# A hybrid decoder layer: moving the adaLN columns along the weight stream, splitting the late ones in halves, and spreading four residuals

## The chip, the cores and the metric

The kernel runs on one core of one Trainium2 chip. The metric is the device time of one execution in microseconds (us), taken as the median of repeated runs. Of its engines the text names TensorE (PE in the profile, with PEld for its weight loads), VectorE (DVE), ScalarE (ACT), GpSimd (POOL) and SyncE (SP), which issues the transfers.

## The reference, cut to what matters

One layer over 256 tokens of width 2048, batch 1. Each of three sub-layers is modulated by a condition vector c:

```python
cond = silu(c)
mod = cond @ ada_w + ada_b            # 9 x 2048 values: shift, scale, gate for three sub-layers
h = ada_in(x, norm_g[0], sh1, sc1)    # rmsnorm(x) * (1 + scale) + shift
x = x + 0.5 * gt1 * swiglu(h, w_gate[0], w_up[0], w_down[0])      # SwiGLU_1, 5632 wide
h = ada_in(x, norm_g[1], sh2, sc2)
x = x + gt2 * hybrid_mixer(h)         # 8 attention heads || 8 gated delta heads, then @ w_out
h = ada_in(x, norm_g[2], sh3, sc3)
x = x + 0.5 * gt3 * swiglu(h, w_gate[1], w_up[1], w_down[1])      # SwiGLU_2
return rmsnorm(x, final_norm)
```

All numbers are float32. With a batch of one, `mod` is a matrix times one vector: 144 groups of 128 outputs, each a sum over 2048 inputs. The kernel calls one such group a **column**.

## The kernel before

**The weight stream.** All weights but `ada_w` are cut into 128x128 tiles, 5392 of them, and packed in the order of use, 8 tiles to a **block**: 674 blocks of 512 KB. `Stream.next` hands out tiles; at the first tile of a block it issues the transfer to `wraw` on SP, the cast to `whi` on ACT (L127, a shorter float type that the PE multiplies fast) and the remainder `wraw - whi` to `wlo` on DVE (L139). Each tile is multiplied as `whi` and `wlo` in turn, so that the product is as good as float32. `wraw`, `whi` and `wlo` have four buffers each; DVE and ACT can be four blocks ahead of the PE and no further. If a `wlo` is late, the PE waits for it.

**The stages, in blocks.** 0 to 111: gate and up products of the first 28 hidden groups of SwiGLU_1 (tile `pgu`, L572 to L574), taken in pieces (`PIECES`), each summing some of the 16 slices of the input over 8 or 4 hidden groups; a piece's partial sums are copied from PSUM by ACT or added into `acc` by DVE (L587), the last ones go to `tg`, `tu` and `hid` (L590, L591, L523, L507). 112 to 167: the down product of that half. 168 to 263: the other half of SwiGLU_1. 264 to 377: the mixer's input projections, with the heads' own small chains of work in between. 378 to 409: the output projection `po` (L492, L493), first four output columns of 128 together (8 blocks), then one after the other (2 blocks each). 410 to 673: SwiGLU_2.

**The columns.** `ada_col` fetches one column of `ada_w` (128x2048, 1 MB, tile `adat`, three buffers at most) and DVE multiplies it with `cs` = silu(c) and sums along the row in one instruction (L264, a custom operation and a read of its accumulator). When columns are fetched is a table, `RATE`: pairs of a block and a number of columns per block from there on. A column is also forced where `ada_need` finds it missing. In SwiGLU_1 the sum follows the fetch in the program at once; in the mixer and later (`W.late`) `total` is put off by two blocks (`owing`, `settle`, `BEHIND`) and placed right after a `wlo`. The first 32 columns are scale and shift of SwiGLU_1: each pair makes one slice of its input ready (`gains` L389, L372, L376 or L383), and the pieces ask for the slices in turn.

**The residuals of the output projection.** When an output column is summed in PSUM, `residual` adds it into `x` in two DVE instructions (L516, L517), `sumsq_add` squares it for the next norm, and `norm2.y` makes the next input from it (a gain L389, an ACT copy, and L416 on DVE). The first four columns do this in one go after the fourth (`after`); the later ones one column late, at the ninth slice of the following one (`LATER`).

**What sets the order.** Each engine takes its instructions strictly in the order that the build gives it; a scheduler lays that order out, so a change of `RATE` reorders DVE, ACT, SP and, around the pieces, the PE. An instruction that waits holds up all that stands behind it on its engine.

## Time and profile before

| what | us |
|---|---|
| median of three runs (lowest, highest) | 1944.64 (1944.19, 1946.02) |
| the profiled execution's own time | 1944.91 |
| its span, first to last instruction | 1943.1 |
| PE busy | 1903.0 |
| PEld busy | 1774.5 |
| DVE busy | 1555.1 |
| ACT busy | 1039.5 |

[...] In the lists of instructions a row has its start, its duration, engine, line, operation, the tile written and those read, and in brackets the idle time of its engine before it with what ended it. Rows of the windows view give for a stretch of time the busy time (and the number of instructions) of PE, PEld, DVE, ACT and POOL, then the granted PE clock, the share of time in which the transfer engines were busy, and GB/s.

### The profile page before, as it was taken

What the parts mean: (1) busy time and instruction counts of PE and PEld (TensorE: products, weight loads), DVE (VectorE), ACT (ScalarE), POOL (GpSimd) and SP (SyncE); (2) the same over time, 40 slices, a digit from 0 to 9 for tenths busy, and PEclk for the clock granted to TensorE, in tenths of its full rate; (3) what the DMA queues carried; (4) which work ended last, traced back from release to release, by engine and by line L of the source; (5) the groups of instructions that cost most, each with busy time, mean ns of one, the idle gap of its engine ahead of it and who ended that gap; (6) DMA issues with size and microseconds to landing.
All of it is one profiled execution on the core that took longest, in us unless ns stands there. A gap on an engine that the chain in (4) does not pass through costs nothing.

```text
span 1943.1 us, 33703 instructions
## 1 busy us (share of the span) xinstructions
PE 1903.0 (98%) x13086; PEld 1774.5 (91%) x13087; DVE 1555.1 (80%) x2414; ACT 1039.5 (53%) x1647; POOL 57.4 (3%) x55
## 2 busy tenths in 40 slices
PE   8999999999999999999999999999999999999998
PEld 7999999988999988889989998999999999999997
DVE  6999888989999997789987989877676765666654
ACT  7433555433455446857757655665554445555553
POOL 0000000000000020000000002100000000000011
PEclk9999999999999999999999999999999999999999
DMA  9998867999989985596567567677777766666663
GB/s 374 350 344 345 294 215 265 400 374 376 361 347 348 349 307 211 197 330 219 204 254 250 207 229 281 206 246 264 240 246 262 244 231 199 203 199 202 200 201 120
DMA packets 129490, 519.58 MB, mean 267 GB/s; under 512 B 18217, under 2 KB 21545, under 8 KB 111153
## 3 DMA queue, kind: packets, MB, share of 16 engines
q1 hardware_dynamic: 129330, 517.42, 74.1%
q8 instruction: 103, 1.69, 0.3%
q14 instruction: 57, 0.47, 0.1%
HBM read 512.89 MB, written 4.47 MB: 266 GB/s over the span
## 4 chain that ended last, share of the span: by engine, by line
PE 77%; DVE 12%; issue 4%; ACT 3%; DMA 2%; SPq 0%; DVEq 0%; ACTq 0%
PE pd L492 12%; PE pu L488 10%; PE pg L488 10%; PE pd L493 6%; PE pu L489 5%; PE pg L489 5%; DVE wlo L139 5%; PE pgu L574 4%; PE pgu L572 4%; PE pgu L573 4%; DVE adat L264 3%; PE po L492 2%; PE pp L795 2%; PE pp L796 2%; PE pp L797 2%
## 5 line engine op out<-in xcount | busy, mean ns | idle before, releaser
L139 DVE TENSOR_TENSOR wlo<-wraw,whi 128x1024 fp32r<-128x1024 f32 x674 | 820.8, 1225 | 263.8 <-ACT whi L127 262.6
L127 ACT CAST whi<-wraw 128x1024 fp32r<-128x1024 f32 x674 | 698.3, 1045 | 509.4 <-PE pd L492 178.1
L492 PE MATMUL pd<-hid,whi 128*128 128x512 f32 x1408 | 462.1, 382 | 0.0
L493 PE MATMUL pd<-hid,wlo 128*128 128x256 f32 x1408 | 384.8, 274 | 2.7 <-DVE wlo L139 2.7
L264 DVE CUSTOM_DVE_ANT_0 adat<-adat,cs,colt 128x2048 f32<-128x2048 f32 x142 | 334.6, 2357 | 7.6 <-DMA adat<-in_ada_dram 7.4
L488 PE MATMUL pg<-hs,whi 128*128 128x512 f32 x912 | 302.1, 382 | 0.5 <-DVE shc L439 0.5
L488 PE MATMUL pu<-hs,whi 128*128 128x512 f32 x912 | 302.2, 382 | 0.0
L492 PEld LDWEIGHTS pd<-hid,whi 128*128 128x128 f32 x1408 | 266.0, 189 | 36.7 <-DVE hid L507 0.2
L493 PEld LDWEIGHTS pd<-hid,wlo 128*128 128x128 f32 x1408 | 270.2, 192 | 6.0 <-DVE wlo L139 5.6
L489 PE MATMUL pu<-hs,wlo 128*128 128x256 f32 x912 | 249.3, 273 | 0.0
L574 PE MATMUL pgu<-hs,wlo 128*128 128x256 f32 x896 | 240.7, 278 | 8.3 <-DVE wlo L139 8.0
L489 PE MATMUL pg<-hs,wlo 128*128 128x256 f32 x912 | 248.8, 273 | 0.0
L572 PE MATMUL pgu<-hs,whi 128*128 128x256 f32 x896 | 244.8, 276 | 0.8 <-DVE acc L587 0.5
L573 PE MATMUL pgu<-hs,whi 128*128 128x256 f32 x896 | 244.5, 276 | 0.0
L488 PEld LDWEIGHTS pg<-hs,whi 128*128 128x128 f32 x912 | 172.4, 189 | 24.9 <-ACT shc L438 0.7
L488 PEld LDWEIGHTS pu<-hs,whi 128*128 128x128 f32 x912 | 172.4, 189 | 23.6
L795 PE MATMUL pp<-hs,whi 128*128 128x256 f32 x656 | 188.4, 288 | 1.1 <-ACT hs L379 1.1
L797 PE MATMUL pp<-hs,wlo 128*128 128x256 f32 x656 | 182.2, 278 | 0.0
L796 PE MATMUL pp<-hs,whi 128*128 128x256 f32 x656 | 181.9, 277 | 0.0
L574 PEld LDWEIGHTS pgu<-hs,wlo 128*128 128x128 f32 x896 | 168.8, 193 | 11.0 <-DVE wlo L139 10.8
L489 PEld LDWEIGHTS pu<-hs,wlo 128*128 128x128 f32 x912 | 175.0, 192 | 1.4 <-DVE wlo L139 1.4
L489 PEld LDWEIGHTS pg<-hs,wlo 128*128 128x128 f32 x912 | 175.1, 192 | 0.3
(335 smaller groups left out, 2585.9 us busy)
## 6 DMA issues: line engine op xcount, KB each, us to landing
wraw<-in_w_dram SPq DMA_DIRECT2D x674, 512.0 KB, 4.4
adat<-in_ada_dram SPq DMA_DIRECT2D x142, 1024.0 KB, 7.5
xr<-in_xr_dram SPq DMA_DIRECT2D x4, 512.0 KB, 5.6
adaf<-in_ada_dram SPq DMA_DIRECT2D x4, 512.0 KB, 8.5
xd<-x SPq DMA_DIRECT2D x4, 512.0 KB, 6.9
rw<-rowd SPq DMA_DIRECT2D x16, 128.0 KB, 4.2
x<-xd SPq DMA_DIRECT2D x4, 512.0 KB, 5.6
out_dram<-o SPq DMA_DIRECT2D x8, 256.0 KB, 2.6
```

The source lines that it names most:

```text
L127: self.cast = self.nc.scalar.copy(self.h, r).ins
L139: lo_ = nc.vector.tensor_tensor(self.l, r, self.h.bitcast(F32), ALU.subtract)
L264: V.tensor_tensor_reduce(t, t, cs, 1.0, L("adab", q, 1), ALU.mult, ALU.add, mod[:, q : q + 1])
L488: PE.matmul(ps, wt[0], both, start=(k == 0), stop=False)
L489: PE.matmul(ps[:, T:], wt[1], part(k, HI), start=False, stop=(k == KD - 1))
L492: PE.matmul(ps, wt[0], act.rearrange("p q (a b) -> p q b a", a=2), start=first, stop=False)
L493: PE.matmul(ps[:, :T], wt[1], woven(act[:, 0]), start=False, stop=last)
L572: PE.matmul(o, wh, part(k, HI), start=first and s == 0, stop=False, skip_group_check=skip)
L573: PE.matmul(o, wh, part(k, LO), start=False, stop=False, skip_group_check=skip)
L574: PE.matmul(o, wl, part(k, HI), start=False, stop=last, skip_group_check=skip)
L795: PE.matmul(pp[i][:, :T], wh, hh, start=(k == 0), stop=False)
L797: PE.matmul(pp[i][:, :T], wl, hh, start=False, stop=(k == KD - 1))
```

## The change

Three things change (the edit inside `total` has no effect, since the late columns no longer pass through it). `RATE` is another table: 0.25 instead of 0.45 columns per block in blocks 28 to 32 and 49 to 55, 0.5 instead of 0.45 in blocks 12 to 27, 33 to 48 and 56 to 65, 0.2 instead of about 0.06 in blocks 66 to 111, none from block 376 to 423 (before: none from 404), and 0.16 instead of 0.125 in SwiGLU_2. A late column is summed in two halves of 1024, the second one block after the first; the first half's sum goes through a small tile `part`. And in the output projection every residual is owed singly: while more than one is owed, two are paid per output column (`SLOTS`, at slices 3 and 11), else one at slice 8.

```diff
-RATE = ((0, 0.5), (12, 0.45), (68, 0.06), (112, 0.5), (168, 0.38), (264, 0.0), (284, 0.26), (404, 0.0), (424, 0.125))
+RATE = ((0, 0.5), (28, 0.25), (33, 0.5), (49, 0.25), (56, 0.5), (66, 0.2), (112, 0.5), (168, 0.38), (264, 0.0), (284, 0.255), (376, 0.0), (424, 0.16))
...
+SLOTS = (3, 11)
...
         def total():
-            with nullcontext() if W.late else W.behind(False):
+            with W.behind(False):
                 V.tensor_tensor_reduce(t, t, cs, 1.0, L("adab", q, 1), ALU.mult, ALU.add, mod[:, q : q + 1])
...
         if W.late:
-            W.owing.append((len(W.order) // WB, total))
+            part = tiny.tile([P, 1], F32, name="part", bufs=4)
+            for i, (start, dst) in enumerate(((L("adab", q, 1), part), (part, mod[:, q : q + 1]))):
+                hf = slice(i * D // 2, (i + 1) * D // 2)
+                W.owing.append((len(W.order) // WB + i, lambda hf=hf, start=start, dst=dst: V.tensor_tensor_reduce(
+                    t[:, hf], t[:, hf], cs[:, hf], 1.0, start, ALU.mult, ALU.add, dst)))
         else:
             total()
...
+            slots = SLOTS if len(owed) > 1 else (LATER,)
...
-                if owed and i == LATER:
+                if owed and i in slots:
                     owed.pop(0)()
...
-            def after(js=js, pj=pj):
-                for q, j in enumerate(js):
-                    residual(pj[q], j, 5, False)
-                    sumsq_add(j)
-                    norm2.y(j)
-                    if j == KD // 2:
-                        sqrt_table(x[:, j, :1])
-
-            if j == 3 or j == KD - 1:
-                after()
-            else:
-                owed.append(after)
+            def after(j, ps):
+                residual(ps, j, 5, False)
+                sumsq_add(j)
+                norm2.y(j)
+                if j == KD // 2:
+                    sqrt_table(x[:, j, :1])
+
+            owed += [lambda j=j, ps=ps: after(j, ps) for j, ps in zip(js, pj)]
+        while owed:
+            owed.pop(0)()
         mx.close()
```

How many columns DVE sums in which stretch of the stream in the two built programs (a column belongs to the block behind whose `wlo` it stands, a halved one to that of its second half):

| blocks | 0-12 | 13-27 | 28-32 | 33-48 | 49-55 | 56-65 | 66-111 | 112-263 | 264-377 | 378-409 | 410-673 |
|---|---|---|---|---|---|---|---|---|---|---|---|
| before | 6 | 7 | 2 | 7 | 3 | 5 | 4 | 62 | 24 | 7 | 15 |
| now | 6 | 8 | 1 | 8 | 2 | 5 | 10 | 61 | 23 | 2 | 16 |

The order moves at many places; three bear the prediction. In the changed program the same source lines stand up to five lines lower (L140 is L139 before, L265 is L264, L381 is L376, L394 is L389, L421 is L416, L521 and L522 are L516 and L517, L592 is L587).

First, DVE from the low part of block 26 to that of block 28, in SwiGLU_1. Before:

```order
L139 TENSOR_TENSOR wlo<-wraw,whi 128x1024
L383 SCALAR_TENSOR_TENSOR hs<-ht,mod,hs 128x2x128
L587 TENSOR_TENSOR acc<-pgu,acc 128x512 x4
L139 TENSOR_TENSOR wlo<-wraw,whi 128x1024
L264 ISA adat,mod<-adat,cs,colt 128x2048
L264 ISA mod 128x1
L587 TENSOR_TENSOR acc<-pgu,acc 128x512 x3
L139 TENSOR_TENSOR wlo<-wraw,whi 128x1024 x2
```

Now:

```order
L140 TENSOR_TENSOR wlo<-wraw,whi 128x1024
L592 TENSOR_TENSOR acc<-pgu,acc 128x512 x4
L140 TENSOR_TENSOR wlo<-wraw,whi 128x1024
L265 ISA adat,mod<-adat,cs,colt 128x2048
L265 ISA mod 128x1
L394 SCALAR_TENSOR_TENSOR g_1253<-mod,colt 128x1
L592 TENSOR_TENSOR acc<-pgu,acc 128x512
L377 SCALAR_TENSOR_TENSOR ht<-x,g_1253,nrow 128x256
L592 TENSOR_TENSOR acc<-pgu,acc 128x512 x2
L140 TENSOR_TENSOR wlo<-wraw,whi 128x1024
L381 TENSOR_TENSOR hs<-ht,hs 128x2x128
```

The column and the seven additions into `acc` stand where they stood; a gain and a product for the next input slice have come in front of block 28, and, as the table counts, one more column lies in the blocks ahead.

Second, DVE from the first of the eight additions that end the third piece to the low part of block 50. Before:

```order
L587 TENSOR_TENSOR acc<-pgu,acc 128x512
L139 TENSOR_TENSOR wlo<-wraw,whi 128x1024
L376 TENSOR_TENSOR hs<-ht,hs 128x2x128
L587 TENSOR_TENSOR acc<-pgu,acc 128x512 x4
L139 TENSOR_TENSOR wlo<-wraw,whi 128x1024
L264 ISA adat,mod<-adat,cs,colt 128x2048
L264 ISA mod 128x1
L587 TENSOR_TENSOR acc<-pgu,acc 128x512 x3
L139 TENSOR_TENSOR wlo<-wraw,whi 128x1024 x3
```

Now:

```order
L140 TENSOR_TENSOR wlo<-wraw,whi 128x1024
L592 TENSOR_TENSOR acc<-pgu,acc 128x512
L265 ISA adat,mod<-adat,cs,colt 128x2048
L265 ISA mod 128x1
L592 TENSOR_TENSOR acc<-pgu,acc 128x512 x4
L140 TENSOR_TENSOR wlo<-wraw,whi 128x1024
L592 TENSOR_TENSOR acc<-pgu,acc 128x512 x3
L140 TENSOR_TENSOR wlo<-wraw,whi 128x1024 x2
```

The low part of block 48 has come out from behind the first addition, which waits for the PE; the column has moved from behind the low part of block 49 to in front of it.

Third, DVE from the low part of block 388 on, where the first four output columns are finished (`g` with a number is the gain of one column). Before, with a second pair of L416, half a residual and a gain still to follow before the low part of block 389:

```order
L139 TENSOR_TENSOR wlo<-wraw,whi 128x1024
L516 SCALAR_TENSOR_TENSOR x<-po,mod,x 128x256 x2
L517 SCALAR_TENSOR_TENSOR x<-po,mod,x 128x256 x2
L516 SCALAR_TENSOR_TENSOR x<-po,mod,x 128x256 x2
L416 SCALAR_TENSOR_TENSOR hs<-x,g_13645,hs 128x2x128
L416 SCALAR_TENSOR_TENSOR hs<-x,g_13654,hs 128x2x128
L517 SCALAR_TENSOR_TENSOR x<-po,mod,x 128x256
L389 SCALAR_TENSOR_TENSOR g_13663<-mod,colt 128x1
L517 SCALAR_TENSOR_TENSOR x<-po,mod,x 128x256
L389 SCALAR_TENSOR_TENSOR g_13672<-mod,colt 128x1
L264 ISA adat,mod<-adat,cs,colt 128x2048
L264 ISA mod 128x1
```

Now:

```order
L140 TENSOR_TENSOR wlo<-wraw,whi 128x1024 x2
L521 SCALAR_TENSOR_TENSOR x<-po,mod,x 128x256 x2
L522 SCALAR_TENSOR_TENSOR x<-po,mod,x 128x256 x2
L521 SCALAR_TENSOR_TENSOR x<-po,mod,x 128x256
L140 TENSOR_TENSOR wlo<-wraw,whi 128x1024
L421 SCALAR_TENSOR_TENSOR hs<-x,g_13716,hs 128x2x128
L421 SCALAR_TENSOR_TENSOR hs<-x,g_13747,hs 128x2x128
L522 SCALAR_TENSOR_TENSOR x<-po,mod,x 128x256
L394 SCALAR_TENSOR_TENSOR g_13779<-mod,colt 128x1
L521 SCALAR_TENSOR_TENSOR x<-po,mod,x 128x256
L394 SCALAR_TENSOR_TENSOR g_13810<-mod,colt 128x1
L140 TENSOR_TENSOR wlo<-wraw,whi 128x1024
```

The low part of block 389 now stands behind five halves of residuals, where it stood behind nine of them, four L416, three gains and a column; the rest of the four residuals is spread over the blocks after it. The two columns that remain in this stage are one at its start (its second half) and one, fetched late, with its halves behind the low parts of blocks 407 and 408.

## The prediction, made before the changed kernel had run

> **What bounds the kernel now.** The page's first line says that the PE is busy for 98% of the span. That leaves 40 us, and a busy PE can still be slowed, so the windows view of the stages comes next (PE, PEld, DVE, ACT, POOL busy, granted clock, share of the transfer engines, GB/s).
>
> ```profile
> PE 1903.0 (98%) x13086; PEld 1774.5 (91%) x13087; DVE 1555.1 (80%) x2414; ACT 1039.5 (53%) x1647; POOL 57.4 (3%) x55
> ...
> 50.00:104.00 54.00, 51.17 (x442) 49.70 (x440) 51.98 (x62) 24.62 (x30) 0.00 (x0) 1.00 0.88 342
> 104.00:168.00 64.00, 59.76 (x528) 59.18 (x528) 61.09 (x71) 25.94 (x30) 0.00 (x0) 1.00 0.93 355
> 212.00:331.00 119.00, 119.00 (x1068) 119.00 (x1067) 95.28 (x154) 64.21 (x95) 0.00 (x0) 1.00 0.70 234
> 331.00:483.00 152.00, 149.90 (x920) 136.76 (x919) 143.28 (x169) 61.96 (x64) 0.00 (x0) 1.00 0.98 382
> 800.00:1168.00 368.00, 358.43 (x2680) 337.25 (x2679) 311.65 (x761) 242.33 (x526) 0.42 (x2) 1.00 0.67 240
> 1275.00:1943.00 668.00, 660.29 (x4043) 606.57 (x4041) 430.28 (x552) 325.74 (x452) 17.95 (x14) 1.00 0.65 217
> ```
>
> From 212 to 331 us, in blocks 66 to 111, the PE does not stop: 1068 matmuls in 119 us, 0.111 us each, 24 to a block, so 2.67 us a block is its own pace. Between 50 and 168 us DVE is busy 113 of 118 us and the PE misses 7: there DVE sets the time. SwiGLU_2, the last row, has a third of DVE free. So the change can earn only where DVE is late, and lose only where it is nearly full.
>
> The waits of the PE by itself, in its list of instructions, show the largest in the output projection:
>
> ```profile
> 1175.48 0.38 PE L492 MATMUL po<-oh,whi 128*128 128x512 f32 x1
> ...
> 1177.10 0.48 PE L492 MATMUL po<-oh,whi 128*128 128x512 f32 x1 [0.69 <-ACT whi L127]
> 1179.59 0.38 PE L493 MATMUL po<-oh,wlo 128*128 128x256 f32 x1 [2.01 <-DVE wlo L139]
> 1179.80 0.59 PE L492 MATMUL po<-oh,whi 128*128 128x512 f32 x1
> ...
> 1182.32 0.63 PE L492 MATMUL po<-oh,whi 128*128 128x512 f32 x1
> ...
> 1183.43 0.38 PE L492 MATMUL po<-oh,whi 128*128 128x512 f32 x1
> ```
>
> The PE stops at 1176.4 (1177.10 less 0.69) and gets the one of block 389 at 1179.6: 0.69 + 2.01 = 2.7 us idle. The 0.69 is put down to a cast, but the next row shows that the low part was missing anyway. What DVE did meanwhile:
>
> ```profile
> 1168.02 1.23 DVE L139 TENSOR_TENSOR wlo<-wraw,whi 128x1024 fp32r<-128x1024 f32 x1 [2.70 <-ACT whi L127]
> 1169.17 0.87 DVE L516 SCALAR_TENSOR_TENSOR x<-po,mod,x 128x256 f32<-128x256 f32 x2
> 1169.95 0.86 DVE L517 SCALAR_TENSOR_TENSOR x<-po,mod,x 128x256 f32<-128x256 f32 x2
> 1170.74 0.87 DVE L516 SCALAR_TENSOR_TENSOR x<-po,mod,x 128x256 f32<-128x256 f32 x2
> ...
> 1173.80 2.40 DVE L264 CUSTOM_DVE_ANT_0 adat<-adat,cs,colt 128x2048 f32<-128x2048 f32 x1
> ...
> 1176.07 1.87 DVE L416 SCALAR_TENSOR_TENSOR hs<-x,g,hs 128x256 fp32r<-128x256 f32 x2
> 1178.32 1.21 DVE L139 TENSOR_TENSOR wlo<-wraw,whi 128x1024 fp32r<-128x1024 f32 x1
> ```
>
> Between the low parts of blocks 388 and 389 lie 9.1 us of residuals, L416 and one column. And from 1179.8 to 1183.4 a matmul of 512 columns takes 0.59 to 0.63 us, where it takes 0.38 before and after. The windows tell why:
>
> ```profile
> 170.00:172.00 2.00, 2.00 (x11) 2.00 (x10) 2.00 (x2) 1.05 (x1) 0.00 (x0) 0.50 0.98 342
> 882.00:886.00 4.00, 4.00 (x37) 4.00 (x37) 3.93 (x11) 3.97 (x6) 0.00 (x0) 1.00 0.99 373
> 1180.00:1182.00 2.00, 2.00 (x7) 1.72 (x7) 2.00 (x3) 0.84 (x2) 1.06 (x1) 0.50 0.70 213
> ```
>
> After the wait the granted clock is 0.50, for some 3.4 us of half the work: 1.7 us more. The same happens at 170 us; behind a wait of 1.58 us that ends at 881.89 (its row is below) it does not.
>
> **The change part by part. Output projection.** The column in front of block 389 goes, and of nine halves of residuals five stay (0.40 us each by the rows above: 2.0 us), so its low part ends near 1169.2 + 2.0 + 1.2 = 1172.4, and the PE asks for it at 1176.8: 4 us early. Behind it come two L416 (1.87 together), two halves (0.8) and two gains (0.3), 3.0 us, then 1.1 for the next low part: 4.1 us to the PE's 2.6 a block. The blocks after that hold one L416, two halves and a gain, 2.9 with their low part, and soon only every other block does. The lead falls to about 2.5 us and then grows, since from 394 on two blocks bring DVE 4.0 us of work in 5.2; it is never used up. So the wait and its slow stretch go: **-2.7 - 1.7 = -4.4 us**. At least -2.7 (if the slow stretch has another cause); no more than -4.4, since nothing else waits there. The late column behind blocks 407 and 408, with a wait for its transfer 4.9 us (by the row at 242.07, below), is paid from the lead won by then, six times 1.2.
>
> **SwiGLU_1, the first two stretches.** Here DVE is full and its list is a sum of durations:
>
> ```profile
> 99.15 1.22 DVE L139 TENSOR_TENSOR wlo<-wraw,whi 128x1024 fp32r<-128x1024 f32 x1
> 100.28 2.35 DVE L264 CUSTOM_DVE_ANT_0 adat<-adat,cs,colt 128x2048 f32<-128x2048 f32 x1
> 102.55 1.88 DVE L587 TENSOR_TENSOR acc<-pgu,acc 128x512 f32<-128x512 f32 x3
> 104.35 2.35 DVE L139 TENSOR_TENSOR wlo<-wraw,whi 128x1024 fp32r<-128x1024 f32 x2
> 105.62 0.38 PE L574 MATMUL pgu<-hs,wlo 128*128 128x256 f32 x1 [2.25 <-DVE wlo L139]
> 157.31 0.69 DVE L587 TENSOR_TENSOR acc<-pgu,acc 128x512 f32<-128x512 f32 x1 [2.19 <-PE pgu L574]
> 157.92 1.22 DVE L139 TENSOR_TENSOR wlo<-wraw,whi 128x1024 fp32r<-128x1024 f32 x1
> 159.39 2.48 DVE L587 TENSOR_TENSOR acc<-pgu,acc 128x512 f32<-128x512 f32 x4
> 161.78 1.21 DVE L139 TENSOR_TENSOR wlo<-wraw,whi 128x1024 fp32r<-128x1024 f32 x1
> 162.91 2.34 DVE L264 CUSTOM_DVE_ANT_0 adat<-adat,cs,colt 128x2048 f32<-128x2048 f32 x1
> 165.19 1.88 DVE L587 TENSOR_TENSOR acc<-pgu,acc 128x512 f32<-128x512 f32 x3
> 166.98 3.48 DVE L139 TENSOR_TENSOR wlo<-wraw,whi 128x1024 fp32r<-128x1024 f32 x3
> 168.25 0.38 PE L574 MATMUL pgu<-hs,wlo 128*128 128x256 f32 x1 [2.25 <-DVE wlo L139]
> DVE acc L587 <- PE pgu L574: 3.4, 3, 2.2
> ```
>
> From start to start a column costs 2.27, an addition 0.6, a low part 1.13. The first waits are at block 28 (105.62) and block 50 (168.25).
>
> Block 28: one column more lies ahead of it (2.27) with a gain and a product (0.2 + 0.4), 2.9 us. DVE's own idle ahead of block 28 pays a part: the last row has three waits for additions, 3.4 us; one, of 2.19, is at 157.31, so 1.2 us lie before. The low part comes 2.9 - 1.2 = 1.7 us later and the PE with it. By block 33 both tables have summed 15 columns and DVE is level again, but the PE, which was at its own pace from 28 to 33, stays 1.7 behind.
>
> Block 50: the first of the eight additions waits for the PE, so it comes at 157.31 + 1.7 = 159.0. From there to the end of the low part of block 50 DVE had 168.2 - 157.3 = 10.9 us to do; now the low part of 48 and L376 are done before, 1.13 + 0.4 less: 9.4. It ends at 168.4, 0.2 later than before. The PE's idle time in blocks 48 to 50 shrinks from 2.4 to about 1.2 us.
>
> Then the clock. Of two waits of 2.25 us one (168.25) was followed by a slow stretch and one (105.62) was not; the windows from 104 to 168 show 1.00. [...] The wait at block 28 grows to about 2.9 us, since the PE loses 1 us of the 1.7 ahead of it: I take a slow stretch there (+1.7) and none at block 50 any more (-1.7); the PE's later arrival only moves block 50's wait forward. Together **+0.2 us**. Bounds: -1.5 with neither, +1.9 with both.
>
> [...]
>
> **SwiGLU_1 from block 66, and the down product.** Ten columns instead of four stand in blocks 66 to 111. Six times 2.27 is 13.6 us of DVE; its row of windows leaves 119 - 95.3 = 23.7. Cover: the PE never waited there, though this happened:
>
> ```profile
> 242.07 2.35 DVE L264 CUSTOM_DVE_ANT_0 adat<-adat,cs,colt 128x2048 f32<-128x2048 f32 x1 [2.58 <-DMA adat<-in_ada_dram]
> ```
>
> DVE stood still for 4.9 us for one column, and the lead held. The down product (331 to 483) has DVE at 94% and the transfer engines at 98%, with as many columns as before, and begins with a smaller lead: I take **+0.5 us**; 0 at best, +3 at worst, more than the 2.1 us that the PE misses there now.
>
> **Mixer and SwiGLU_2.** A half costs 1.28 us (the kernel's first columns are summed so):
>
> ```profile
> L710 DVE CUSTOM_DVE_ANT_0 adaf<-adaf,cs,colt x2: 1276/1280/1284, 11.7 to 14.8; 128x1024 f32<-128x1024 f32 x2
> 881.89 0.30 PE L1215 MATMUL pft<-colt,on 128*128 128x128 f32 x1 [1.58 <-issue]
> ```
>
> Two halves take some 0.3 us more than one whole (2 x 1.28 against 2.35, with another read of 0.08): 12 us over 40 columns, hidden in the 56 us that DVE has free from 800 to 1168 and the 238 of SwiGLU_2. Without that cover each would cost its 0.3. What stands behind a late column on DVE waits 1.2 us less. The wait at 881.89 is one for attention's `on`, whose chain on DVE stands behind a column in block 307: **-1.2 us**, if that is all that makes it late; 0 to -2.5 with the other chains.
>
> **The sum**: -4.4 + 0.2 + 0.5 - 1.2 = -4.9. From the profiled execution's 1944.9 that is 1940.0; it lies 0.3 above the median, so the forecast is **1939.7 us**. What this kernel's measurement can tell from no change is about 0.2%, 3.9 us, so 1940.7 is the edge of faster.
>
> **The rivals.** [...]
>
> *Slow at both places and no gain in the mixer*: +1.7 and +1.2 on the forecast, 1942.6. For it: the wait at 881.89 is named "issue" and not DVE.
>
> *The new columns of blocks 66 to 111 wait for their transfers*: if all six cost 2.27 + 2.58 = 4.85, they want 29.1 us of the 23.7 that DVE has free; the PE loses 5.4 and, stopping at each of the last three, three slow stretches of 1.7: 1939.7 + 10.5 = 1950.2, slower than before. It decides from the point where the lead of four blocks is gone, in the last of these blocks, where an L590 group stands in nearly each. Against it: one of four waited so.
>
> *The wait of block 389 only moves*, to 390 or 391, where the low parts stand behind 2.9 us: a stop of 1 us with a slow stretch, +2.7, 1942.4.
>
> [...]
>
> *The change doesn't do what it says*: the columns taken out are forced back in by `ada_need` at the projection's end; the built order has one such, so this is small: 1944.
>
> **Chances.** Forecast 0.42, no slow stretch at 28 0.25, slow at both 0.14, transfers 0.08, moved wait 0.05, page's rule 0.03, undone 0.03. The forecast's own range is 1938 to 1941.5. The range that leaves out about 2 in 10 runs from 1935.5 (the mixer's lower bound with neither slow stretch) to 1943.0 (above the third case). Faster by over 0.2%: nearly all of the second case and five sixths of the first, 0.60; slower: 0.08; within: 0.32.
>
> **What would show it.** Right: no PE wait over 0.5 us and a clock of 1.00 in the output projection; the low part of block 28 near 107 us, that of block 50 near 168; no PE wait from 212 to 331 us; the wait before `pft` near block 307 down to about 0.4. Wrong: a wait of the PE for `wlo` in blocks 389 to 395, a half clock there, PE waits in blocks 95 to 115, or a low part of block 28 that comes no later than 105.6.

## The result, and the profile after

The changed kernel is slower: 1949.2 us (median of 17 runs, 1945.5 to 1953.7) against 1944.64 for the kernel before, whose 17 runs beside it lay between 1941.3 and 1946.3. The ratio is 1.0024, with a 95% interval from 1.0017 to 1.0030. The forecast was 1939.7, in a range from 1935.5 to 1943.0.

The page of the changed kernel has the same 98% of PE as before; what differs is the sum by engine of the chain of waits, and the group of the whole columns (busy time, mean ns, idle time before them):

```profile
PE 1903.0 (98%) x13086; PEld 1776.8 (91%) x13087; DVE 1564.0 (80%) x2496; ACT 1041.6 (53%) x1645; POOL 57.0 (3%) x55
...
PE 74%; DVE 11%; DMA 6%; issue 4%; ACT 3%; SPq 0%; DVEq 0%; ACTq 0%
...
L265 DVE CUSTOM_DVE_ANT_0 adat<-adat,cs,colt 128x2048 f32<-128x2048 f32 x101 | 239.0, 2366 | 18.0 <-DMA adat<-in_ada_dram 18.0
```

Transfers have gone from 2% to 6% of the chain, and DVE stands 18.0 us in front of columns that have not landed (7.4 before, though of 142 columns and not of 101). PE's busy time is to the tenth that of before: all 7.4 us by which the span grew (1950.5 against 1943.1) are idle time of the PE. The profiled execution of the changed kernel took 1952.3 us, 3.1 more than the median, so the stretches below add up to 7.4 us where the medians differ by 4.6. Where the idle time is shows when the moment at which the PE first uses the low part of a block is compared in the two traces. Differences of the changed kernel to the one before, in us, by stretch of blocks (the start of the execution apart, since it moves by up to 2.4 us from one execution to the next):

| stretch | what runs | forecast | measured |
|---|---|---|---|
| start | | | -0.3 |
| 0 to 66 | SwiGLU_1, first stretches | +0.2 | -0.8 |
| 66 to 120 | SwiGLU_1, first down blocks | | **+11.7** |
| 120 to 264 | down product, second half | +0.5 (from 66 on) | +0.3 |
| 264 to 384 | mixer | -1.2 | +1.6 |
| 384 to 408 | output projection | -4.4 | -5.0 |
| 408 to end | SwiGLU_2 | 0 | -0.1 |

The windows that answer to those of before (same columns: PE, PEld, DVE, ACT, POOL busy, clock, share of the transfer engines, GB/s), the third of them over blocks 66 to 111:

```profile
49.70:103.70 54.00, 51.54 (x442) 49.82 (x440) 53.14 (x63) 23.51 (x29) 0.00 (x0) 1.00 0.91 344
103.70:167.70 64.00, 60.28 (x522) 59.90 (x522) 59.29 (x70) 26.33 (x30) 0.00 (x0) 0.97 0.84 326
211.00:345.80 134.80, 126.18 (x1105) 125.12 (x1104) 110.26 (x171) 67.31 (x99) 0.00 (x0) 0.99 0.74 266
341.00:494.00 153.00, 149.13 (x908) 135.44 (x908) 144.76 (x171) 62.16 (x64) 0.00 (x0) 1.00 0.98 384
```

The stretch in which the PE never stopped now takes 134.8 us with 8.6 idle and a clock of 0.99, while DVE has 24 us free. So it is not too little room on DVE; it is when DVE is free. Its list, and that of the PE, give the stops one by one:

```profile
252.78 2.35 DVE L265 CUSTOM_DVE_ANT_0 adat<-adat,cs,colt 128x2048 f32<-128x2048 f32 x1 [0.89 <-DMA adat<-in_ada_dram]
265.33 2.35 DVE L265 CUSTOM_DVE_ANT_0 adat<-adat,cs,colt 128x2048 f32<-128x2048 f32 x1 [2.37 <-DMA adat<-in_ada_dram]
281.02 2.35 DVE L265 CUSTOM_DVE_ANT_0 adat<-adat,cs,colt 128x2048 f32<-128x2048 f32 x1 [3.72 <-DMA adat<-in_ada_dram]
285.24 0.38 PE L579 MATMUL pgu<-hs,wlo 128*128 128x256 f32 x1 [1.66 <-DVE wlo L140]
296.93 2.35 DVE L265 CUSTOM_DVE_ANT_0 adat<-adat,cs,colt 128x2048 f32<-128x2048 f32 x1 [3.92 <-DMA adat<-in_ada_dram]
301.14 0.38 PE L579 MATMUL pgu<-hs,wlo 128*128 128x256 f32 x1 [2.24 <-DVE wlo L140]
312.97 2.35 DVE L265 CUSTOM_DVE_ANT_0 adat<-adat,cs,colt 128x2048 f32<-128x2048 f32 x1 [3.66 <-DMA adat<-in_ada_dram]
317.52 0.38 PE L579 MATMUL pgu<-hs,wlo 128*128 128x256 f32 x1 [1.09 <-DVE wlo L140]
329.15 2.35 DVE L265 CUSTOM_DVE_ANT_0 adat<-adat,cs,colt 128x2048 f32<-128x2048 f32 x1 [2.46 <-DMA adat<-in_ada_dram]
333.36 0.38 PE L579 MATMUL pgu<-hs,wlo 128*128 128x256 f32 x1 [2.17 <-DVE wlo L140]
345.89 0.38 PE L498 MATMUL pd<-hid,wlo 128*128 128x256 f32 x1 [1.56 <-DVE wlo L140]
```

A column every four or five blocks (one more, at 239.85, waited 0.97 and is not listed); the wait of DVE grows from 0.9 to 3.9 us, and from the column at 281.02 on each one reaches the PE: 1.66 + 2.24 + 1.09 + 2.17 = 7.2 us. A last wait of 1.56, at block 112, stands behind a column that had landed in time: by then there was no lead left. Together 8.7 us. After the second of the PE's waits, at 301.14, comes a slow stretch (clock 0.50 at 303, below; from 302.1 to 305.5 the matmuls start 0.21 us apart instead of 0.11), 1.7 us more, which makes 10.4 of the 11.7; no row names the rest.

Where the wait comes from is to be seen on SP and DVE around the column at 296.93 (SPq rows: the issue of transfers; x3 are three in a row):

```profile
285.21 3.34 SPq L125 DMA_DIRECT2D wraw<-in_w_dram  x3
288.60 0.43 SPq L261 DMA_DIRECT2D adat<-in_ada_dram  x1
```

```profile
286.97 1.23 DVE L140 TENSOR_TENSOR wlo<-wraw,whi 128x1024 fp32r<-128x1024 f32 x1
...
288.78 1.22 DVE L140 TENSOR_TENSOR wlo<-wraw,whi 128x1024 fp32r<-128x1024 f32 x1
...
291.78 1.23 DVE L140 TENSOR_TENSOR wlo<-wraw,whi 128x1024 fp32r<-128x1024 f32 x1 [0.52 <-ACT whi L128]
296.93 2.35 DVE L265 CUSTOM_DVE_ANT_0 adat<-adat,cs,colt 128x2048 f32<-128x2048 f32 x1 [3.92 <-DMA adat<-in_ada_dram]
```

The fetch stands on SP behind the transfer of block 100, and that one waits for a raw buffer which DVE frees with the low part of block 95 (286.97 + 1.23 = 288.2; each fifth block has a raw buffer of its own in this stage, so there are five of `wraw` and not four). So the fetch cannot leave before 288.6, whatever SP does. The sum stands on DVE behind the low part of block 97, two low parts on, and DVE is there at 293.0, 4.4 us after the issue. The transfer lands 8.3 us after it (296.9), and DVE stands for the difference, 3.9 us.

The wait grows because the transfers take longer, and not because DVE comes sooner: from the issue to the end of DVE's work ahead of the sum it is 4.6 us at 252.78 and 4.4 at 281.02 and 296.93, while the transfer takes 5.5, 8.1 and 8.3. Nor does a full lead help much: with 5.9 us of it DVE reached the sum at 242.07 in the kernel before 5.6 us after the issue, against a transfer of 8.2, and with 5.8 us the one at 284.37 in k11_dose (below) after 4.3, against 7.6. What stretches the transfers from 5.5 to 8.3 us no run here shows. That DVE stood for nothing is an idle time; that it stood ahead of a low part is the loss.

### The profile page after: what moved, and what is told of

Its sections match the earlier page's. It is cut to its first block, busy times and chain, and to the rows that moved or that the text cites. A ratio compares the mean times of both kernels' runs of the same rounds, so it can differ in the third digit from the quotient of the medians.

```text
span 1950.5 us, 33806 instructions
## 1 busy us (share of the span) xinstructions
PE 1903.0 (98%) x13086; PEld 1776.8 (91%) x13087; DVE 1564.0 (80%) x2496; ACT 1041.6 (53%) x1645; POOL 57.0 (3%) x55
## 4 chain that ended last, share of the span: by engine, by line
PE 74%; DVE 11%; DMA 6%; issue 4%; ACT 3%; SPq 0%; DVEq 0%; ACTq 0%
PE pd L497 14%; PE pg L493 10%; PE pu L493 10%; PE pd L498 7%; PE pu L494 5%; PE pg L494 5%; DVE wlo L140 4%; PE po L497 3%; DMA adat<-in_ada_dram 3%; PE pgu L579 2%; PE pgu L577 2%; PE pgu L578 2%; PE pp L800 2%; PE pp L801 2%; PE pp L802 2%
## 5 line engine op out<-in xcount | busy, mean ns | idle before, releaser
L140 DVE TENSOR_TENSOR wlo<-wraw,whi 128x1024 fp32r<-128x1024 f32 x674 | 821.5, 1226 | 255.6 <-ACT whi L128 253.1
L493 PE MATMUL pu<-hs,whi 128*128 128x512 f32 x912 | 302.1, 382 | 0.0
L579 PE MATMUL pgu<-hs,wlo 128*128 128x256 f32 x896 | 241.4, 279 | 14.7 <-DVE wlo L140 14.3
L265 DVE CUSTOM_DVE_ANT_0 adat<-adat,cs,colt 128x2048 f32<-128x2048 f32 x101 | 239.0, 2366 | 18.0 <-DMA adat<-in_ada_dram 18.0
```

Of the source, the lines that this page charges most:

```text
L140: lo_ = nc.vector.tensor_tensor(self.l, r, self.h.bitcast(F32), ALU.subtract)
L265: V.tensor_tensor_reduce(t, t, cs, 1.0, L("adab", q, 1), ALU.mult, ALU.add, mod[:, q : q + 1])
L493: PE.matmul(ps, wt[0], both, start=(k == 0), stop=False)
L579: PE.matmul(o, wl, part(k, HI), start=False, stop=last, skip_group_check=skip)
```

## The experiments

Twelve kernels ran, each timed in several rounds beside the kernel before, whose median in these rounds was 1944.9, 1945.7 and 1945.5 us. The last columns give the difference to the kernel before by stretch of blocks, from one profiled execution each; in the mixer (264 to 384) they depend on which slow stretches of the clock (0.50 for some 3.4 us, as from 302.1 to 305.5 above), 1.7 us each, that execution had.

| run | median, us | ratio (95%) | 0-66 | 66-120 | 120-264 | 264-384 | 384-408 |
|---|---|---|---|---|---|---|---|
| changed kernel | 1949.2 | 1.0024 (1.0017 to 1.0030) | -0.8 | +11.7 | +0.3 | +1.6 | -5.0 |
| k1_put_off | 1948.9 | 1.0020 (1.0011 to 1.0028) | -0.8 | +11.7 | +0.3 | +0.3 | -5.0 |
| k7_put_off | 1941.7 | 0.9983 (0.9974 to 0.9992) | -1.0 | +2.9 | +0.5 | -3.4 | -5.0 |
| k13_put_off_hole | 1941.7 | 0.9981 (0.9972 to 0.9990) | -0.9 | 0.0 | -1.9 | +1.0 | -5.0 |
| k2_rate66 | 1936.9 | 0.9962 (0.9949 to 0.9974) | -0.8 | 0.0 | -0.5 | -3.3 | -5.0 |
| k11_dose | 1941.7 | 0.9978 (0.9969 to 0.9988) | -0.8 | +1.3 | -0.6 | +2.1 | -5.0 |
| k12_whole | 1948.8 | 1.0019 (1.0009 to 1.0029) | -0.9 | +9.9 | +0.4 | -2.2 | -5.0 |
| k3_residuals | 1945.4 | 1.0002 (0.9993 to 1.0010) | 0.0 | 0.0 | 0.0 | +0.8 | -0.4 |
| k4_out_of_po | 1940.0 | 0.9976 (0.9966 to 0.9987) | 0.0 | +0.2 | 0.0 | -1.6 | -5.0 |
| k5_halves | 1945.4 | 1.0002 (0.9994 to 1.0011) | +0.9 | 0.0 | +0.1 | -2.1 | +0.5 |
| k6_first | 1943.8 | 0.9999 (0.9990 to 1.0008) | -0.9 | +0.3 | -0.6 | +0.8 | -0.3 |
| k9_col28 | 1937.2 | 0.9960 (0.9948 to 0.9972) | -3.9 | 0.0 | -2.0 | +2.6 | -5.0 |
| k10_best | 1933.0 | 0.9939 (0.9926 to 0.9953) | -3.9 | 0.0 | -2.0 | -0.6 | -5.0 |

### Where the sum stands: k1_put_off, k7_put_off, k13_put_off_hole

The first try at putting the sums off, on the changed kernel:

```diff
+        elif m > 1 and len(W.order) // WB < 112:
+            W.owing.append((len(W.order) // WB, lambda: V.tensor_tensor_reduce(...)))
         else:
             total()
```

> The changed kernel, with one thing altered: below block 112 the sum of a column that is not needed yet stands two blocks behind its fetch on DVE, as the late columns' sums do, instead of right at its fetch. Same columns, same places of the fetches, same DVE work. Theory A (each of the new columns of blocks 66 to 111 holds DVE up because it stands on DVE ahead of the landing of its own transfer, about 3.5 us a column): DVE's waits for adat in 212 to 331 us go from 18 us to under 4, the PE's five waits of 1.1 to 2.2 us in blocks 93 to 112 and the half clock at 302 us go, and 10 to 11 us come back: 1938 to 1940. Theory B (DVE has simply too much work there, six columns more of 2.3 us): the waits for adat go but the PE still waits for low parts: no more than 3 us come back, 1946 or more. Theory C (the transfers themselves are late because the queue is full, wherever the sum stands): DVE still waits for adat, only later: 1944 to 1949.

It measured 1948.9, and the waits of the changed kernel are there again. But it tells nothing of the theories: `both` calls `ada_need` at each tile, and that ends with `W.settle()`, which pays all owed sums at once, so the order of DVE was that of the changed kernel. It is of use as a repeat: the same order gave the same 11.7 us, though made up otherwise. The PE waited 7.3 us instead of 8.7 and had two slow stretches instead of one, the second after this wait, which was 2.17 in the changed kernel:

```profile
333.61 0.58 PE L582 MATMUL pgu<-hs,wlo 128*128 128x256 f32 x1 [3.11 <-DVE wlo L140]
```

The wait of 1.56 at block 112 is not there in this execution. That fits a PE that is soon to wait for DVE anyway: what a slow stretch takes from it is then not lost a second time. The mixer has +0.3 instead of +1.6, so 1.3 us there is what one execution differs from another; its wait for `x` before `plog` is 1.34 us here and 2.81 in the changed kernel.

The second try takes that call away where only the first 32 columns can be asked for:

```diff
             ada_col()
-        W.settle()
+        if m > 1:
+            W.settle()
```

> The changed kernel with the sums of blocks 66 to 111 really put off (the run k1_put_off built the order of the changed kernel: an earlier call pays all owed sums at the next tile). Each column is fetched where it was, but its sum stands five low parts later on DVE (behind the low part of block 97 before, now of 102). Same columns, same DVE work, 5 of 9 columns of the stretch still summed there. Theory A (the loss is the standing of the sum ahead of its transfer's landing): DVE's waits for adat from 212 to 331 us fall from 18 us to under 2, no PE wait over 0.5 us in blocks 90 to 112, no half clock at 302 us, 11 to 12 us less than the changed kernel: 1937 to 1939. Theory B (six columns of 2.3 us are too much work): PE waits for low parts stay in blocks 100 to 112, 1944 or more.

The waits are gone, with the same columns in the same places on SP. Windows of this kernel over blocks 66 to 111, and of its end alone, then DVE and the PE one by one:

```profile
211.00:334.00 123.00, 123.00 (x1104) 123.00 (x1103) 108.39 (x169) 67.64 (x99) 0.00 (x0) 1.00 0.81 291
```

```profile
288.66 2.35 DVE L276 CUSTOM_DVE_ANT_0 adat<-adat,cs,colt 128x2048 f32<-128x2048 f32 x1
...
328.41 2.35 DVE L265 CUSTOM_DVE_ANT_0 adat<-adat,cs,colt 128x2048 f32<-128x2048 f32 x1 [0.71 <-DMA adat<-in_ada_dram]
```

```profile
340.04 0.38 PE L502 MATMUL pd<-hid,wlo 128*128 128x256 f32 x1 [2.60 <-DVE wlo L140]
```

DVE does 108.4 us of work in 123 and the PE does not stop once: theory B, too much work, falls, and so does theory C, since DVE waits for a column for no more than the 0.7 us of the row at 328.41. The transfers issued between 270 and 311 us are a little shorter here than in the changed kernel (6.2 to 7.2 us against 8.1 to 8.4), but in the next run, where those issued between 270 and 300 take 8.1 to 8.8, DVE does not wait for them either. What is left is 2.9 us behind block 112, where two columns stand behind the low parts of neighbouring blocks (111 and 112) at the start of the down product. Against the changed kernel the median is 7.5 us lower. The expectation of 11 to 12 was missed: within blocks 66 to 112 all 11.6 us came back, but 2.9 were lost again behind them. To see whether the two columns make the 2.9, the third run leaves blocks 107 to 116 without any:

```diff
-(66, 0.2), (112, 0.5), (168, 0.38), (264, 0.0), (284, 0.255)
+(66, 0.2), (107, 0.0), (117, 0.5), (168, 0.38), (264, 0.0), (284, 0.315)
```

> k7_put_off without columns from block 107 to 116, the mixer at 0.315 to take them over. In k7_put_off two columns stood behind the low parts of 111 and 112, where the down product begins, and the PE waited 2.6 us at block 113. Without them that wait goes, and 66 to 120 costs the PE nothing: 2.5 to 3 us less than k7_put_off: 1938 to 1939.5 by the median, if the mixer takes its columns as it did in k2_rate66.

They do: in the window of this kernel from 211 to 340 us the PE has no gap,

```profile
211.00:340.00 129.00, 129.00 (x1148) 128.71 (x1147) 113.92 (x180) 72.27 (x106) 0.00 (x0) 1.00 0.79 276
```

but the median, 1941.7, did not follow. The mixer, which has to take five columns more, came out 4.4 us worse than in k7_put_off in the profiled executions, and blocks 120 to 264 2.3 better. In the mixer it has a slow stretch at 864 us that k7_put_off did not have and one at 745 that is twice as long; together they are 3.4 us, as much as k7_put_off's whole gain there. The expectation that it would go as in k2_rate66 was wrong.

### How many columns: k2_rate66, k11_dose

```diff
-(66, 0.2), (112, 0.5), (168, 0.38), (264, 0.0), (284, 0.255)
+(66, 0.06), (112, 0.5), (168, 0.38), (264, 0.0), (284, 0.33)
```

> The changed kernel, with the rate of columns in blocks 66 to 111 back at 0.06 and the mixer's raised from 0.255 to 0.33 to take the columns over. Theory A (the loss is these six columns alone): the 11.6 us that are lost in blocks 92 to 112 come back, and the mixer pays for six more halved columns up to 2 us: 1937 to 1940. Theory B (the loss comes from what the first stretches leave behind for blocks 66 to 111, a smaller lead): the waits in blocks 93 to 112 stay, 1946 to 1950.

1936.9, and 0.0 in blocks 66 to 120: the 11.7 us are the columns that were added, and nothing that the earlier stretches leave behind. The mixer takes them for nothing here. The dose between:

```diff
-(66, 0.2), (112, 0.5), (168, 0.38), (264, 0.0), (284, 0.255)
+(66, 0.125), (112, 0.5), (168, 0.38), (264, 0.0), (284, 0.29)
```

> The changed kernel with a column every 8 blocks (0.125) instead of every 5 (0.2) in blocks 66 to 111, the rest in the mixer (0.29 instead of 0.255); the sums stand ahead of their transfers as in the changed kernel. If a stop of DVE (2.3 us of sum and up to 3.7 us of waiting) is paid back at about 0.8 us a block, 8 blocks pay it and 5 do not: the PE then waits in blocks 66 to 112 for less than 1 us in all and 10 to 12 us come back: 1936 to 1940. If any wait for adat of 2 us and more reaches the PE, half of the loss stays: 1943 to 1945.

DVE still stands in front of its columns, and the PE does not notice (two rows of DVE, then the window):

```profile
284.37 2.35 DVE L265 CUSTOM_DVE_ANT_0 adat<-adat,cs,colt 128x2048 f32<-128x2048 f32 x1 [3.29 <-DMA adat<-in_ada_dram]
304.76 2.35 DVE L265 CUSTOM_DVE_ANT_0 adat<-adat,cs,colt 128x2048 f32<-128x2048 f32 x1 [2.17 <-DMA adat<-in_ada_dram]
```

```profile
211.00:334.00 123.00, 123.00 (x1103) 122.97 (x1102) 101.10 (x161) 65.35 (x97) 0.00 (x0) 1.00 0.74 259
```

The lead of DVE, from the end of a low part to its first use, tells why (us, best before a stop and least behind it, from the two traces; four stops in a row, in the changed kernel from that at 239.85, in k11_dose from that at 262.50):

| | first | second | third | fourth |
|---|---|---|---|---|
| changed kernel, every 5 blocks | 5.3 to 1.6 | 5.4 to 2.7 | 4.7 to 0.5 | 3.8, PE waits 1.7 |
| k11_dose, every 8 blocks | 5.8 to 1.5 | 5.8 to 1.1 | 5.8 to 1.1 | 4.3 to 0.4 |

A stop costs some 3 to 5 us of lead, and the blocks up to the next one win back 2 to 4 where there are five, and all of it, to the full 5.8, where there are eight, but for the last (4.3). By the median k11_dose came out at 1941.7, above the 1936 to 1940 expected: 1.3 us went up to block 120, 0.9 of it in a wait at block 115, and the mixer lost 2.1.

### The output projection: k3_residuals, k4_out_of_po

The first has the columns of the kernel before and the residuals one by one, that is the last three pieces of the change alone; the second the residuals in one go and the columns out, that is a table alone:

```diff
# k3_residuals, on the kernel before
+            slots = SLOTS if len(owed) > 1 else (LATER,)
...
+            owed += [lambda j=j, ps=ps: after(j, ps) for j, ps in zip(js, pj)]
# k4_out_of_po, on the kernel before
-(284, 0.26), (404, 0.0), (424, 0.125)
+(284, 0.33), (376, 0.0), (424, 0.16)
```

> The kernel before, with the residuals of the output projection owed one by one and nothing else: its columns as before, whole and in the projection too. If the wait of block 389 came from the residuals standing in one go (4 us of them ahead of the low part), it goes with its slow stretch, and 4 to 5 us are won: 1940. If the column of 2.3 us ahead of block 389 is needed for the wait, about half of the wait stays: the low part of 389 comes some 2 us earlier, the PE still waits 0.5 to 1 us, with or without a slow stretch: 1941 to 1943.5.

> The kernel before with a table that has no columns from block 376 to 423 and 0.33 instead of 0.26 in the mixer; whole columns, residuals in one go. It asks what the columns alone do in the output projection, where the residuals alone gave 0.4 us (k3_residuals: a wait of 2.0 moved to block 384 and one of 0.9 came at block 395). By the prediction's sum for block 389 (9.1 us of DVE work between two low parts, 2.3 of them a column) the column alone takes the wait of 2.7 us down to 0.4: -2.3 to -4 in blocks 384 to 408. If both parts are needed, under -1.5. In the mixer, whole columns at 0.33 show whether the 3.3 us that k2_rate66 wins from block 264 to 384 come from the rate (then they are here too) or from the halves (then not).

The waits of the PE around that stage, k3_residuals first (all rows), then k4_out_of_po (the only row), as time in all, times, longest:

```profile
PE pft L1216 <- DVE on L1212: 2.0, 1, 2.0
PE po L494 <- DVE wlo L140: 1.3, 2, 0.9
PE pot L1160 <- DVE orw L1151: 0.4, 1, 0.4
```

```profile
PE pfo L1199 <- ACT x L1195: 0.4, 1, 0.4
```

The residuals alone win 0.4 us: the wait leaves block 389, but a column then stands ahead of attention's last `on` (2.0) and of block 395 (0.9). The columns alone win the whole 5.0, more than the 2.3 to 4 expected and to the hundredth as much as both together (-4.98 in each), and the kernel as a whole gains 0.24%. In this stage the new order of the residuals was not needed. The mixer with whole columns at a rate of 0.33 is 1.6 us better than before; k2_rate66 with halves is 3.3 better, of which 1.7 is a slow stretch at 808 us (clock 0.50 from 808 to 810 in the kernel before) that it was spared.

### The halves: k5_halves, k12_whole

The first puts only the halving into the kernel before, the second takes only the halving out of the changed one:

```diff
# k5_halves, on the kernel before (and the reverse for k12_whole, on the changed kernel)
-            W.owing.append((len(W.order) // WB, total))
+            part = tiny.tile([P, 1], F32, name="part", bufs=4)
+            for i, (start, dst) in enumerate(((L("adab", q, 1), part), (part, mod[:, q : q + 1]))):
...
+                W.owing.append((len(W.order) // WB + i, lambda hf=hf, start=start, dst=dst: V.tensor_tensor_reduce(...)))
```

> The kernel before with the late columns summed in two halves a block apart and nothing else. The prediction's step has -1.2 us in the mixer (the wait of 1.58 at 881.9 shrinks to 0.4); the trace of the changed kernel has +1.2 there, that of k2_rate66, with another rate, -3.3. If the halves help by themselves: -1 to -3 from block 264 to 384. If what a rate does to the places of the columns decides, and not the halves: within 1 of the kernel before, and the wait at 881.9 stays.

> The changed kernel with the late columns summed whole, two blocks behind their fetch, as in the kernel before; nothing else. If halving pays in the mixer, this is slower than the changed kernel by 1 to 3 us from block 264 to 384; if it is worth nothing, the two are within 1 us there once the slow stretches of 1.7 us are counted apart. The loss in blocks 88 to 112 stays at 11 to 12 us: 1947 to 1951.

k5_halves is 2.1 us better in the mixer, but 1.7 of it is again the slow stretch at 808 us that this execution did not have (clock 1.00 from 808 to 810), and by the median it is the kernel before (1.0002). k12_whole has +9.9 in blocks 66 to 120 and -2.2 in the mixer where the changed kernel has +1.6; it too was spared a slow stretch. With 1.3 us between two executions of one order, these runs show no gain from halving, and if anything a small loss. The wait that it was meant to shorten stands in the changed kernel as before (in the order of time it comes second):

```profile
PE plog L1184 <- ACT x L1272: 2.8, 1, 2.8
...
PE pft L1220 <- issue: 1.6, 1, 1.6
```

In k5_halves it is down to 0.17, and a wait of 1.10 before `pvq`, 7 us later, is new:

```profile
876.77 0.54 PE L1219 MATMUL pft<-colt,on 128*128 128x128 f32 x2 [0.17 <-PE pp L801]
```

The places differ: the kernel before sums a column behind the low part of block 307, k5_halves its halves behind 307 and 308, the changed kernel, with another rate, behind 306 and 307. With whole columns at 305 and 308 (k4_out_of_po, k10_best) the wait is gone, with one at 306 (k12_whole) it is 1.61. So the wait seems to hang on where the column stands, and the new table to have moved the halves to where it is as long as before; no run moved that column alone. What sets the wait of 2.8 for `x` was not tried.

### The first stretches: k6_first, k9_col28, k10_best

k6_first is the kernel before with the new table up to block 65:

```diff
-(0, 0.5), (12, 0.45), (68, 0.06)
+(0, 0.5), (28, 0.25), (33, 0.5), (49, 0.25), (56, 0.5), (66, 0.06)
```

> The kernel before, with the changed table of rates for blocks 0 to 65 alone (whole columns, residuals in one go, from block 66 on as before). The prediction's step has +0.2 us (a slow stretch moves from block 50 to block 28, bounds -1.5 to +1.9): 1944.8. The trace of the changed kernel has the PE 1.1 us ahead at block 52, with a slow stretch at 107.5 us and none at 170: 1943.5. If the five-block waits in 240 to 330 us come from these stretches and not from the six new columns, 1950 or more.

By stretch it is the gain of the changed kernel again (-0.9), and less than 1 us either way in each later stretch; by the median no change can be told (0.9999). k9_col28 is k2_rate66 with one column moved:

```diff
-(0, 0.5), (28, 0.25), (33, 0.5)
+(0, 0.5), (26, 0.34), (32, 0.5)
```

> k2_rate66 with the one column that stands between the low parts of blocks 27 and 28 moved behind that of block 28 (0.34 from block 26 instead of 0.25 from block 28, 0.5 from block 32). If the wait of 2.7 us at block 28 is this column and the gain and product behind it, it goes, with the half clock at 109 us: 2 to 4.4 us less than k2_rate66, less what comes back at block 49: 1933 to 1936. If DVE is simply full up to block 50, the wait only moves to blocks 29 to 35 and the end stays at 1936 to 1937.

The wait at block 28 went, with its slow stretch: -3.9 up to block 66, 3.1 better than k2_rate66, and 1.5 more in blocks 120 to 264. But the mixer's columns stand one block off in it, and there came two slow stretches, at 805.6 and 1037.7 us, that k2_rate66 did not have: no gain by the median. The last one sums its late columns whole, which gives the mixer nearly the order that k4_out_of_po has (its edit on k9_col28 is that of k12_whole):

> k9_col28 with its late columns whole instead of halved: the first stretches of k9_col28 (3.9 us better than the kernel before by block 56), the mixer's columns two blocks behind their fetch at 0.33, as in k4_out_of_po (1.6 better from block 264 to 384), none in the output projection (5.0 better). The sum is 10.5 less than the kernel before in its own profiled execution, 1934 to 1935. If halves are worth something, no better than k9_col28: 1936 to 1938.

1933.0 us, 0.9939 of the kernel before (0.9926 to 0.9953): 12 us, the best of all and better than both kernels. Of these, 8.9 are the first stretches and the output projection. The mixer gave 0.6 where 1.6 was expected, and 2.0 came from blocks 120 to 264, where nothing was expected: that the sum came near the expected 1934 to 1935 is in part luck. Those 2.0 are won little by little and were not followed up. Its window from 103.7 to 167.7 (the PE misses 0.2 us; 4.2 in the kernel before from 104 to 168, 3.7 in the changed one) and its waits for low parts in SwiGLU_1 (14.3 in the changed kernel):

```profile
103.70:167.70 64.00, 63.84 (x554) 62.35 (x552) 62.77 (x74) 27.11 (x32) 0.00 (x0) 1.00 0.91 350
```

```profile
PE pgu L575 <- DVE wlo L140: 4.1, 8, 0.8
```

## Why the prediction was wrong

**The step that failed** is the cover for the new columns in blocks 66 to 111: "DVE stood still for 4.9 us for one column, and the lead held", taken as +0.5 with +3 as the worst. The row at 242.07 was read rightly: DVE was ready for that column 2.6 us before it landed, and the sum itself makes up the rest of the 4.9. What it was taken to prove does not follow. The lead held, but barely: in that trace it goes from 5.9 us at block 78 to 0.5 at block 79, is 3.9 at block 84 and 5.8 again only at block 86. No other column came for 17 blocks, and k11_dose shows that 8 are about enough to win a stop back; the new table has one every 5, and the changed kernel and k7_put_off show that there the lead runs out, and that it is the place of the sum, not its 2.27 us, that costs. The free 23.7 us of DVE were a share over the stretch; each stop is paid from 5.8 us of lead and from what the next few blocks give.

The loss was among the rivals, as six columns that wait for their transfers: 1950.2 us. Its price per column, 2.58 us of waiting, is also the mean that was measured (18.0 over 7), but the single waits go from 0.9 to 3.9. Its three slow stretches and 5.4 of waiting (10.5) stand against one and 8.7 here, so that its total is so near is in part luck. It got 0.08 because only one of the four columns before had waited so. But two of these four stood at the edges of the stretch, and the order of SP and DVE told more than their count: from block 87 on each of the new columns is fetched behind the transfer of a block three ahead of the low part behind which it is summed, as the one at 242.07 was, against a transfer of 8.2 us. The order alone does not settle it: the column at 285.39 before was fetched three ahead too, with a transfer of 6.2 us, and waited 0.1.

**Output projection**: -4.4 forecast, -5.0 measured, the mechanism right: the wait and the slow stretch both went; the window of the changed kernel over that stage has no gap and a clock of 1.00:

```profile
1180.00:1230.00 50.00, 50.00 (x308) 45.95 (x307) 45.85 (x71) 32.64 (x47) 13.95 (x12) 1.00 0.69 225
```

The term was mis-sized by 0.6; by estimate 0.4 of it is lost work beside the 2.7 us between records. At full clock a record of 0.38 us is followed by the next start after 0.22 (1183.43 and 1183.65 in the kernel before), so the idle times of 0.69 and 2.01, behind records of 0.38 and 0.48, are 0.85 and 2.27 of delay. The working, though, shared the credit between column and residuals: k4_out_of_po gets it all from the columns, and k3_residuals 0.4 from the residuals.

**SwiGLU_1, first stretches**: +0.2 forecast, -0.8 measured. The slow stretch did come after the wait at block 28 (2.72 us, at 106.64, expected near 107; clock 0.50 from 108 to 110) and none came at block 50 (1.00 from 166 to 174), as forecast. By block 32 the PE was 3.0 us behind, 1.3 and the slow stretch's 1.7 (1.7 and 1.7 forecast). But it did not stay so: it won back 0.7 by block 40 and 0.4 by block 48, and then its wait at block 49 was 1.0 us. At its use of block 50 it was 0.8 behind, where the forecast had 0.2 and the slow stretch, 1.9. What was mis-sized is the delay that was carried on. The +1.7 at block 28 and the -1.7 at block 50 were the author's choice: no run shows what decides whether a wait is followed by a slow stretch. Over the profiled executions one followed the wait of 2.72 us at block 28 8 times in 8, and that of 1.0 at block 49 not once in 8.

**Mixer and SwiGLU_2**: -1.2 forecast, +1.6 measured (+0.3 in a second execution of the same order). The step that failed is that half a column in place of a whole one takes 1.2 us off the `pft` wait, whatever else moves: it is 1.6 us as before. In k5_halves, with the old table, it did shrink, to 0.17, and a wait of 1.10 came behind it; the new table set the halves behind 306 and 307 instead, which seems to be why. The term reckoned with no move and with nothing behind.

**The slow stretches**: that the one at 1180 us has another cause than the wait, the case behind the lower bound of -2.7, falls. It went with its wait in every kernel without a column there: each gained 5.0 us in this stage, where the wait alone is 2.7 us (3.1 by the estimate above), and from 1160 to 1210 k4_out_of_po has no gap and a clock of 1.00, as the changed kernel above. But a wait is not enough for a slow stretch: k5_halves waits 2.86 us at the same place and has none (clock 1.00 from 1180 to 1182, below).

**The range**: its lower end does not come out of its own terms. With neither slow stretch and the mixer's lower bound they give -4.4 - 1.5 + 0.5 - 2.5 = -7.9, that is 1936.7 and not 1935.5. Nothing hangs on it, since the miss is at the other end.

## What to carry to other kernels

An in-order engine that may run a few blocks ahead has its lead as its account: price a stop against that lead and against what is won back until the next stop, not against the free share of a stretch. For every sum that waits for a transfer, look on both engines at what stands between the issue and the use: where the issue itself waits for the engine that will use the data, what that engine does in between is all that covers the transfer (4.3 to 6.2 us in the traces here, against transfers of 5.3 to 8.4). Putting the use a few blocks later won back nearly all here (11.7 us to 2.9); making these sums smaller was not tried. And when several edits are made at once, run each alone: here the table of rates held both the gain of 5.0 us and the loss of 11.7, and by the medians the two other edits were worth nothing that could be told.

## What the hardware showed that was not expected

The granted clock was 0.50 for some 3.4 us after waits of 2.25 us (at 168.25 in the kernel before, slow from 169.5 to 172.9) and 2.72 us (at 106.64 in the changed one, 107.5 to 110.9), and the same wait in the same order of instructions was hit, that is followed by such a slow stretch, in one execution and spared in another. Up to block 66 k5_halves is instruction for instruction the kernel before; its wait, and the windows behind it in k5_halves and in the kernel before:

```profile
105.46 0.58 PE L578 MATMUL pgu<-hs,wlo 128*128 128x256 f32 x1 [2.26 <-DVE wlo L139]
```

```profile
106.00:108.00 2.00, 2.00 (x12) 2.00 (x11) 2.00 (x2) 0.00 (x0) 0.00 (x0) 0.50 0.80 268
```

```profile
106.00:108.00 2.00, 2.00 (x20) 2.00 (x20) 2.00 (x2) 0.40 (x1) 0.00 (x0) 1.00 0.72 207
```

Over the profiled executions: a wait of 2.25 us at block 28 was hit 1 time in 4, one of 2.25 at block 50 4 in 4, one of 2.72 at block 28 8 in 8, one of 1.0 at block 49 0 in 8, and in the changed kernel 2.24 (block 98) was hit and 2.17 (block 108) not:

```profile
303.00:305.00 2.00, 2.00 (x12) 2.00 (x11) 2.00 (x4) 1.24 (x2) 0.00 (x0) 0.50 0.81 238
```

The wait at block 389, in two parts of about 0.7 and 2.0 us, was hit in the kernel before and in k6_first and spared in k5_halves, although its second part was a little longer there:

```profile
1178.63 0.38 PE L497 MATMUL po<-oh,wlo 128*128 128x256 f32 x1 [2.19 <-DVE wlo L139]
```

```profile
1180.00:1182.00 2.00, 2.00 (x14) 1.84 (x14) 2.00 (x3) 0.01 (x2) 0.69 (x1) 1.00 0.96 393
```

Each takes 1.7 us of the PE's work (3.4 us at 0.50). How much of that is left at the end of a stage differs: in k5_halves the one at block 28 had become 0.9 by block 40, and the two in k1_put_off came to no more than the one in the changed kernel. So a wait of 2.25 us with its slow stretch comes to up to 4.0 us (2.25 + 1.7, an estimate), and part of the spread between runs of one kernel may be nothing else; that was not tried.
